# A down projection made of seven quarter products instead of eight, with VectorE summing the weights

## The chip, the cores and the metric

The kernel runs on one core of one Trainium2 chip. The metric is the device time of one execution in microseconds (us). Five engines work side by side, each through its own queue in order: TensorE (PE, matrix products), VectorE (DVE), ScalarE (ACT), GpSimd (POOL) and SyncE (SP), which here issues all the transfers.

## The reference, cut to what matters

One decoder layer on 512 tokens of 1024 channels: a combined projection, retention, dilated attention, a gated mix, an output projection, then the part that is changed:

```python
u = rmsnorm(x, g_mlp) @ w_up                  # w_up:   1024 x 4096
x = x + jnp.square(jax.nn.relu(u)) @ w_down   # w_down: 4096 x 1024
gate_p = jax.nn.sigmoid(rmsnorm(x, g_ple) @ w_ple_gate)
return x + gate_p * (p_i @ w_ple_proj)
```

All is float32.

## The kernel before

Every large product is made of three: each operand is split exactly into two parts of type float32r, `hi` and `lo`, and `mm3` issues hi·hi, hi·lo and lo·hi into one PSUM bank. One `mm3` is three matmuls of 128 x 128 stationary against 512 moving columns (fp32r), each with its own weight load (PEld in the profile).

**Weights.** `make_plan` lists 0.5 MB units of weights in the order of use. `fetch` takes a buffer of the pool `wraw` (three of them) and issues the transfer on SP. `split_unit` makes `whi` (ACT, a copy, L186) and `wlo` (DVE, raw minus whi, L187), both from the pool `wsp`, which has four buffers of each. `units(n)` hands out n units and has two more split ahead (`AHEAD`). So a unit's ACT copy waits until PE has left the unit four before it, and a transfer waits until an earlier unit's `wlo` has been made.

**The tail.** `tail` runs the output projection (w_o), then eight steps f of 512 hidden channels. Step f makes the up projection in two panels of 256 channels (`cols_gemm`: weights stationary, h2, the normed tokens, moving; 48 matmuls for two units), and then the down projection of step f-1 (`rows_gemm`, twice, for 512 output columns each: hidden values `uh`, `ul` stationary, weights moving; 48 matmuls for two units). So the values of a step are used one step after they are made. The function `act` turns a PSUM bank of 128 channels into hidden values: relu on ACT, times itself on DVE, `uh` on ACT, `ul` on DVE. A finished down bank is added to the tokens `x` by DVE (`add`, L835), one bank of 128 tokens x 512 columns at a time. In the last step the tokens go on into `norm_T` as they come: squares with row sums on ACT, a power on POOL, a scaling on DVE (`y`), four PE transposes each for two halves, and for each 128 channels a scaled copy on ACT (`h3h`) and a difference on DVE (`h3l`). The gate product (w_ple_gate) reads these.

**Order.** The code is recorded by a framework that schedules the instructions of each engine by their priority and by when buffers come free, so the size of a pool can move instructions anywhere in the program. Transposes of the norm are put into a list with a lag and are issued between steps of products (`later`, `tick`).

**Memory.** Large tiles come from `bigp`, 16 buffers of 128 x 2048 floats. PSUM has two pools of four banks, `psg` (`gbank`) and `psa` (`bank`).

Of the kernel before, what the change touches and what calls it, by code (L numbers as in the profile page):

```python
# [71 lines left out]
def R(ap):  # L72
    return ap.bitcast(F32R)


class Block:
    """One decoder layer on one core."""

    def __init__(self, ctx, tc, a):
        self.tc, self.nc, self.a = tc, tc.nc, a  # L80
        pool = lambda n, b, **k: ctx.enter_context(tc.tile_pool(name=n, bufs=b, **k))
        self.const = pool("const", 1)
        self.wraw = pool("wraw", 3)
# [17 lines left out]
    def later(self, lag, fn, key=None):  # L101
# [44 lines left out]

# [1 line left out]
    AHEAD = 2  # L148

    def plan_rows(self, w, c0, nk, r0=0):  # L150
        for u in range(nk // 2):
            self.plan.append((w[r0 + 256 * u : r0 + 256 * (u + 1), c0 : c0 + 512], 2 * u if w is self.w_in else None))

    def plan_cols(self, w, c0, nk):
# [3 lines left out]
    def fetch(self, n):  # L158
        while len(self.raws) < min(len(self.plan), n):
            src, g0 = self.plan[len(self.raws)]  # L160
            raw = self.wraw.tile([P, 1024], F32, tag="raw", name=self.nm("raw"))
            k = src.shape[0] // P
            raw = raw.rearrange("p (k n) -> p k n", k=k)
            self.nc.sync.dma_start(raw, src.rearrange("(k p) n -> p k n", p=P))
            self.raws.append((raw, g0))

    def ahead(self, n):
        while len(self.loaded) < min(len(self.plan), self.used + n):
            self.fetch(len(self.loaded) + 1)
            self.loaded.append(self.split_unit(*self.raws[len(self.loaded)]))  # L170

# [6 lines left out]
    def split_unit(self, raw, g0):  # L178
        """raw weights (times the gain of their input channel) as the exact sum of two float32r parts"""
        nc = self.nc  # L180
        k = raw.shape[1]
        hi = self.wsp.tile([P, 1024], F32, tag="whi", name=self.nm("whi")).rearrange("p (k n) -> p k n", k=k)
        lo = self.wsp.tile([P, 1024], F32, tag="wlo", name=self.nm("wlo")).rearrange("p (k n) -> p k n", k=k)
        if g0 is None:
            for i in range(k) if self.pinned else [slice(0, k)]:
                self.pin(nc.scalar.activation(R(hi[:, i]), raw[:, i], AF.Copy))  # L186
                nc.vector.tensor_tensor(R(lo[:, i]), raw[:, i], hi[:, i], op=ALU.subtract)  # L187
        else:
            for i in range(k):
                g = self.gcol[:, g0 + i : g0 + i + 1]  # L190
                self.pin(nc.scalar.activation(R(hi[:, i]), raw[:, i], AF.Copy, scale=g))  # L191
# [23 lines left out]

    def mm3(self, ps, sh, sl, mh, ml, first, last):
        t = self.nc.tensor
        t.matmul(ps, sh, mh, start=first, stop=False)  # L218
        t.matmul(ps, sh, ml, start=False, stop=False)  # L219
        t.matmul(ps, sl, mh, start=False, stop=last)  # L220
# [91 lines left out]

# [1 line left out]
    def rstd(self, ss, w, count):  # L314
# [47 lines left out]

# [1 line left out]
    def setup(self):  # L364
# [62 lines left out]

# [1 line left out]
    def embed(self, norm):  # L429
# [31 lines left out]

# [215 lines left out]

# [1 line left out]
    def ret_proj(self, extra=None):  # L679
# [97 lines left out]

# [1 line left out]
    def mix(self, A, O):  # L779
# [43 lines left out]

# [1 line left out]
    def tail(self, mx):  # L825
# [21 lines left out]
        h3 = None  # L847
        us = {}
        for f in range(NF + 1):
            if f < NF:  # L850
                u = self.new_act(1, "u")
                us[f] = u

                def act(n, ps):
                    r, q = self.tmp("ur"), self.tmp("uq")
                    nc.scalar.activation(r, ps, AF.Relu)
                    nc.vector.scalar_tensor_tensor(q, ps, 0.0, r, op0=ALU.max, op1=ALU.mult)
                    hi, lo = u[0][0][:, n], u[1][0][:, n]
                    nc.scalar.activation(R(hi), q, AF.Copy)
                    nc.vector.tensor_tensor(R(lo), q, hi, op=ALU.subtract)  # L860

                if f == 0:
                    self.cols_gemm_halves(h2, KD, act, lambda t: self.force(("h2", t, 1)))
                else:
                    for c in range(2):
                        self.cols_gemm(h2, KD, lambda n, ps: act(2 * c + n, ps))
            if f == 2:
# [4 lines left out]
            if f > 0:  # L872
                ub = us.pop(f - 1)
                for half in range(2):
                    cons = add(half)
                    if f == NF and half == 1:
                        h3 = self.new_act(2, "h3")

                        def cons(t, ps):
                            add(1)(t, ps)  # L880
                            self.norm_T(xs[t], t, 24, h3, "h3", 3)
                    self.rows_gemm(ub, 4, cons)

# [12 lines left out]
    def make_plan(self):  # L896
# [9 lines left out]
        for half in range(2):  # L906
            self.plan_rows(a["w_o"][0], 512 * half, KD)
        for f in range(NF + 1):
            if f < NF:
                for c in range(2):  # L910
                    self.plan_cols(a["w_up"][0], 512 * f + 256 * c, KD)
            if f > 0:
                for half in range(2):
                    self.plan_rows(a["w_down"][0], 512 * half, 4, 512 * (f - 1))
        for half in range(2):
# [37 lines left out]
```

## Time and profile before

| what | value |
| --- | --- |
| median of 3 runs | 1062.81 us (1061.33 to 1064.92) |
| profiled execution, first to last instruction (span) | 1058.8 us |
| PE busy in the span | 1033.6 us (98%) |
| DVE, ACT, POOL busy | 587.3, 425.5, 137.7 us |
| granted TensorE clock, mean | 0.998 |
| read from HBM, written | 98.61 MB, 4.21 MB |
| tail with the eight steps | from about 652 to 1008 us of the span |

The record gives the profiled execution by its span; its time as a run is not listed beside it. The median of the runs is 4.0 us above the span. A profile line names the line of the code, the engine, the operation, what is written and read (buffer numbers left out), the shape, and how many; then the busy time, the mean of one in ns, and the idle time of the engine just before, with what ended it. An x and a count after an engine's time is the number of instructions. A timeline line has the start and the duration in us.

### The profile page before, as it was taken

Reading aid. Unit: us, or ns where it says so; the run is one execution under the profiler, and the core shown is the slowest. Engines: PE = TensorE matmul, PEld = TensorE weight load, DVE = VectorE, ACT = ScalarE, POOL = GpSimd, SP = SyncE. Lnnn points to the kernel's source line nnn. Section 1 sums busy time; section 2 is a strip of 40 time slices with the busy share of each in tenths; the row PEclk is TensorE's granted clock in tenths of the full one; section 3 lists DMA queues with packets and bytes.
Section 4 is the critical chain, followed back from the end, with each engine's and each line's share of the span. In section 5 each row is a group of like instructions: output and inputs, shape, how many; then the busy total and the mean of one; then the engine's idle time right before and its main releaser. Section 6 shows DMA issues by size and latency. Waiting matters only on the chain.

```text
span 1058.8 us, 12846 instructions
## 1 busy us (share of the span) xinstructions
PE 1033.6 (98%) x4906; PEld 866.1 (82%) x4906; DVE 587.3 (55%) x929; ACT 425.5 (40%) x948; POOL 137.7 (13%) x126
## 2 busy tenths in 40 slices
PE   8898989999998999999999999999999999999998
PEld 6776879989986888888888888988888888888887
DVE  5588767677578635545443436554444545445573
ACT  6444545555533334435333325532232332332351
POOL 0254034033025301010100100000000000000000
PEclk9999999999999999999999999999999999999999
DMA  8432312223221322212234332225232332323221
GB/s 305 133 114 72 94 41 80 80 80 100 80 80 40 119 80 74 86 60 86 93 100 133 135 107 72 91 82 197 80 119 80 99 101 85 114 88 110 81 80 59
DMA packets 71708, 103.64 MB, mean 98 GB/s; under 512 B 5808, under 2 KB 38624, under 8 KB 71648
## 3 DMA queue, kind: packets, MB, share of 16 engines
q1 hardware_dynamic: 71648, 102.83, 30.8%
q8 instruction: 38, 0.62, 0.2%
q14 instruction: 22, 0.18, 0.1%
HBM read 98.61 MB, written 4.21 MB: 97 GB/s over the span
## 4 chain that ended last, share of the span: by engine, by line
PE 82%; DVE 6%; issue 2%; POOL 2%; ACT 1%; DMA 1%; DVEq 0%; ACTq 0%; POOLq 0%
PE pg L218 25%; PE pg L219 25%; PE pg L220 25%; DVE ro L472 2%; DVE wlo L192 1%; PE ph L484 1%; POOL r L317 1%; PE pt L327 1%; POOL mt L667 1%; PE po L600 1%; PE sc L577 1%; DVE ro L474 1%; PE ry L762 1%; DVE zn L520 1%; DMA raw<-in_w_up 1%
## 5 line engine op out<-in xcount | busy, mean ns | idle before, releaser
L218 PE MATMUL pg<-whi,hh 128*128 128x512 f32 x480 | 201.0, 419 | 3.2 <-ACT whi L191 2.2
L219 PE MATMUL pg<-wlo,hh 128*128 128x512 f32 x480 | 189.0, 394 | 1.7 <-DVE wlo L192 1.6
L220 PE MATMUL pg<-whi,hl 128*128 128x512 f32 x480 | 189.1, 394 | 0.0
L186 ACT ACTIVATE whi<-raw 128x1024 fp32r<-128x1024 f32 (+1 forms) x96 | 99.8, 1041 | 177.0 <-PE pg L220 117.0
L187 DVE TENSOR_TENSOR wlo<-raw,whi 128x1024 fp32r<-128x1024 f32 (+1 forms) x96 | 118.4, 1235 | 87.6 <-ACT whi L186 86.7
L192 DVE SCALAR_TENSOR_TENSOR wlo<-raw,gcol,whi 128x512 fp32r<-128x512 f32 (+1 forms) x184 | 122.2, 705 | 64.3 <-ACT whi L191 64.1
L191 ACT ACTIVATE whi<-raw,gcol 128x512 fp32r<-128x512 f32 (+1 forms) x184 | 107.6, 640 | 90.2 <-PE pg L220 51.4
L317 POOL TENSOR_TENSOR r<-v,mhalf 128x1 f32<-128x1 f32 (+1 forms) x52 | 40.4, 777 | 672.3 <-DVE v L316 672.3
L218 PEld LDWEIGHTS pg<-whi,hh 128*128 128x128 f32 x480 | 98.5, 205 | 17.9 <-ACT whi L191 2.8
L219 PEld LDWEIGHTS pg<-wlo,hh 128*128 128x128 f32 x480 | 99.0, 206 | 16.8 <-DVE wlo L192 3.3
L220 PEld LDWEIGHTS pg<-whi,hl 128*128 128x128 f32 x480 | 98.3, 205 | 17.4 <-DVE hl L341 0.4
L218 PE MATMUL pg<-h2h,whi 128*128 128x512 f32 (+1 forms) x288 | 105.7, 367 | 1.7 <-ACT h2h L335 1.7
L219 PE MATMUL pg<-h2l,whi 128*128 128x512 f32 (+1 forms) x288 | 105.3, 366 | 0.0
L220 PE MATMUL pg<-h2h,wlo 128*128 128x512 f32 (+1 forms) x288 | 105.2, 365 | 0.0
L218 PE MATMUL pg<-whi,uh 128*128 128x512 f32 x256 | 99.9, 390 | 0.0
L220 PE MATMUL pg<-whi,ul 128*128 128x512 f32 x256 | 99.6, 389 | 0.0
L219 PE MATMUL pg<-wlo,uh 128*128 128x512 f32 x256 | 99.6, 389 | 0.0
L835 DVE TENSOR_TENSOR x<-x,pg 128x512 f32<-128x512 f32 x72 | 49.4, 686 | 65.3 <-PE pg L220 65.1
L218 PEld LDWEIGHTS pg<-h2h,whi 128*128 128x128 f32 x288 | 54.3, 188 | 10.7 <-ACT h2h L335 1.9
L219 PEld LDWEIGHTS pg<-h2l,whi 128*128 128x128 f32 x288 | 54.3, 189 | 8.9 <-DVE h2l L336 0.2
L220 PEld LDWEIGHTS pg<-h2h,wlo 128*128 128x128 f32 x288 | 54.3, 188 | 8.7
L220 PEld LDWEIGHTS pg<-whi,ul 128*128 128x128 f32 x256 | 48.0, 188 | 10.0
(159 smaller groups left out, 1644.3 us busy)
## 6 DMA issues: line engine op xcount, KB each, us to landing
raw<-in_w_in SPq DMA_DIRECT2D x76, 512.0 KB, 3.7
raw<-in_w_up SPq DMA_DIRECT2D x32, 512.0 KB, 3.8
raw<-in_w_down SPq DMA_DIRECT2D x32, 512.0 KB, 3.5
raw<-in_w_ret_out SPq DMA_DIRECT2D x8, 512.0 KB, 3.5
raw<-in_w_o SPq DMA_DIRECT2D x8, 512.0 KB, 3.4
raw<-in_w_ple_gate SPq DMA_DIRECT2D x8, 512.0 KB, 3.5
x<-in_x SPq DMA_DIRECT2D x8, 256.0 KB, 6.5
pp_dram<-pp SPq DMA_DIRECT2D x8, 256.0 KB, 3.5
```

Source lines behind the costliest of these rows:

```text
L186: self.pin(nc.scalar.activation(R(hi[:, i]), raw[:, i], AF.Copy))
L187: nc.vector.tensor_tensor(R(lo[:, i]), raw[:, i], hi[:, i], op=ALU.subtract)
L191: self.pin(nc.scalar.activation(R(hi[:, i]), raw[:, i], AF.Copy, scale=g))
L192: nc.vector.scalar_tensor_tensor(R(lo[:, i]), raw[:, i], g, hi[:, i], op0=ALU.mult, op1=ALU.subtract)
L218: t.matmul(ps, sh, mh, start=first, stop=False)
L219: t.matmul(ps, sh, ml, start=False, stop=False)
L220: t.matmul(ps, sl, mh, start=False, stop=last)
L317: self.nc.gpsimd.tensor_tensor(r, v, self.mhalf[:, :w], op=ALU.pow)
L327: nc.tensor.transpose(ps[:, k * P : (k + 1) * P], part[:, k * P : (k + 1) * P], self.ident)
L472: nc.vector.tensor_tensor(v4(t2)[:, :, o0 : o0 + 64], v4(zn)[:, :, i0 : i0 + 64], bc(Sn[:, o0 : o0 + 64], 64), op=ALU.mult)
L474: nc.vector.tensor_tensor(o, t1, t2, op=ALU.add)
L835: nc.vector.tensor_tensor(v, v, ps, op=ALU.add)
```

## The change

The loop over eight steps becomes a loop over four of 1024 hidden channels. The up projection of a step is four panels of 256 channels as before, in another order. Its down projection is 512 tokens x 1024 channels times 1024 channels x 1024 columns; both operands are halved both ways, and the four quarters of the result are put together from seven quarter products (a scheme of the Strassen kind, in Winograd's form) in place of eight. Each quarter product is 256 tokens x 512 channels x 512 columns, 24 matmuls, for two units of weights.

The left sides are made by `seven_left` once for each 128 channels of half a step: with z the four squared quarters, four DVE differences (one of 512 elements, three of 256), one ACT copy and one DVE difference of 1792 elements for hi and lo. The right sides are weight units; products 4, 3, 7 and 6 need the sum of two quarters (two transfers and a DVE sum for each unit, L205), product 1 the difference of two units that are already loaded (L202), products 5 and 2 a plain unit. So a step's down projection loads 20 units of `w_down` where it loaded 8, makes 14 units where it had 8, and DVE makes 10 sums or differences of 128 x 1024. The order of the units is m4 m3 m5 m4 m3 m5, m2 m2, m1 m1, m7 m7, m6 m6, with two PE banks for each, and products 2, 7 and 6 are summed onto the banks of 4, 5 and 3. The banks go into `x` by 18 DVE additions of 128 x 512 per step; there were 16 for the same channels. The relu is squared by ACT (it was a DVE product). Down now follows up directly within a step. `wraw` has six buffers in place of three; the scratch for dynamic transfers is made smaller.

```diff
-        self.wraw = pool("wraw", 3)
+        self.wraw = pool("wraw", 6)
...
+    def seven_left(self, z, a21, U, j):
+        sub = lambda o, x, y: nc.vector.tensor_tensor(o, x, y, op=ALU.subtract)
+        sub(z[:, 2], z[:, 1], z[:, 0])
+        sub(z[:, 3:5], z[:, 0:2], z[:, 7:8].to_broadcast([P, 2, 256]))
+        sub(z[:, 5], a21, z[:, 7])
+        sub(z[:, 6], a21, z[:, 1])
...
+        nc.scalar.activation(R(hi), src, AF.Copy)
+        nc.vector.tensor_tensor(R(lo), src, hi, op=ALU.subtract)
...
     def ahead(self, n):
...
+            if isinstance(src, tuple) and src[0] is None:
+                self.nc.vector.tensor_tensor(raw, raw, self.raws[g0][0], op=ALU.subtract)
+                g0 = None
+            elif isinstance(src, tuple):
+                self.nc.vector.tensor_tensor(raw, raw, g0, op=ALU.add)
+                g0 = None
+            self.loaded.append(self.split_unit(raw, g0))
...
+    def seven_gemm(self, U, xs, ready):
...
+        for u in range(2):
+            for m in (4, 3, 5):
+                product(m, m, u, u == 0, u == 1)
+        m4 = []
+        for p in range(2):
+            t = self.tmp("m4")
+            nc.scalar.activation(t, banks[4, p], AF.Copy)
+            m4.append(t)
+            acc(X(0, 1, p), banks[3, p])
+            acc(X(0, 1, p), banks[5, p], ALU.subtract)
+        for u in range(2):
+            product(2, 4, u, False, u == 1)
+        for p in range(2):
+            acc(X(1, 0, p), banks[4, p])
+            acc(X(1, 1, p), banks[4, p], ALU.subtract)
+        for u in range(2):
+            product(1, 1, u, u == 0, u == 1)
+        for p in range(2):
+            acc(m4[p], banks[1, p])
+            acc(X(0, 0, p), m4[p])
+            acc(X(1, 1, p), m4[p])
+        for u in range(2):
+            product(7, 5, u, False, u == 1)
+        for p in range(2):
+            acc(X(0, 0, p), banks[5, p])
+            if ready is not None:
+                ready(p)
+        for u in range(2):
+            product(6, 3, u, False, u == 1)
+        for p in range(2):
+            acc(X(1, 1, p), banks[3, p])
+            if ready is not None:
+                ready(2 + p)
...
-        for f in range(NF + 1):
+        for f in range(NF // 2):
...
+            self.seven_gemm(U, xs, ready)
```

How it moves instructions, at three places. First VectorE's queue in a down projection, before, from the first addition of a down projection of 512 channels into its second half of columns:

```order
L835 TENSOR_TENSOR x_5176<-x_5176,pg_7448 128x512
L860 TENSOR_TENSOR ul_7287<-uq_7431,uh_7286 128x512
L835 TENSOR_TENSOR x_5176<-x_5176,pg_7462 128x512
L835 TENSOR_TENSOR x_5177<-x_5177,pg_7476 128x512
L187 TENSOR_TENSOR wlo_7507<-raw_7504,whi_7506 128x1024
L835 TENSOR_TENSOR x_5177<-x_5177,pg_7490 128x512
L187 TENSOR_TENSOR wlo_7513<-raw_7510,whi_7512 128x1024
L835 TENSOR_TENSOR x_5176<-x_5176,pg_7516 128x512
```

and in the changed kernel, at the end of a down projection, products 1, 7 and 6 (`m_` is the copy of product 4, `raw` a weight unit, `pb` and `pg` banks):

```order
L900 TENSOR_TENSOR x_5177<-x_5177,m_7388 128x512
L224 TENSOR_TENSOR wlo_7486<-raw_7480,whi_7485 128x1024
L205 TENSOR_TENSOR raw_7501<-raw_7501,raw_7503 128x1024
L900 TENSOR_TENSOR x_5176<-x_5176,pb_7316 128x512
L900 TENSOR_TENSOR x_5176<-x_5176,pb_7323 128x512
L224 TENSOR_TENSOR wlo_7507<-raw_7501,whi_7506 128x1024
L224 TENSOR_TENSOR wlo_7527<-raw_7524,whi_7526 128x1024
L224 TENSOR_TENSOR wlo_7545<-raw_7542,whi_7544 128x1024
```

Between two banks' additions now stand sums of weights and splits, and the split of product 6's second unit (`wlo_7507`) stands behind the additions of product 7's banks.

Second, PE's queue where the last down projection ends and the gate product begins, before (`uh` hidden values, `pt` transposes of `y`, `h3h` and `h3l` the gate's left side):

```order
L218 MATMUL pg_8068<-whi_7866,uh_7572 128x512
L219 MATMUL pg_8068<-wlo_7867,uh_7572 128x512
L220 MATMUL pg_8068<-whi_7866,ul_7573 128x512
L327 MATMUL pt_8110<-ident,y_8051 128x128 x4
L218 MATMUL pg_8135<-whi_7932,h3h_7926 128x512
L219 MATMUL pg_8135<-wlo_7933,h3h_7926 128x512
L220 MATMUL pg_8135<-whi_7932,h3l_7928 128x512
```

and now:

```order
L256 MATMUL pg_7928<-whi_8134,uh_7565 128x512
L257 MATMUL pg_7928<-wlo_8135,uh_7565 128x512
L258 MATMUL pg_7928<-whi_8134,ul_7569 128x512
L256 MATMUL pg_8301<-whi_8184,h3h_7888 128x512
L257 MATMUL pg_8301<-wlo_8185,h3h_7888 128x512
L258 MATMUL pg_8301<-whi_8184,h3l_7890 128x512
L256 MATMUL pg_8301<-whi_8184,h3h_7888 128x512
L257 MATMUL pg_8301<-wlo_8185,h3h_7888 128x512
L365 MATMUL pt_8244<-ident,y_8178 128x128 x4
```

Before, `pt_8110` is the third token tile's first half, and all transposes of the first two tiles stand ahead of it; now the gate's first matmul stands ahead of `pt_8244`, which is the first half of the second tile.

Third, the head of SP's queue, before:

```order
L384 DMA x_91<-in_x 128x512 x2
L164 DMA raw_98<-in_w_in 128x2x512
L384 DMA x_91<-in_x 128x512 x2
L164 DMA raw_102<-in_w_in 128x2x512
L372 DMA rows<-in_ret_gn 8x128
```

and now:

```order
L189 DMA raw_98<-in_w_in 128x2x512
L422 DMA x_91<-in_x 128x512 x2
L189 DMA raw_102<-in_w_in 128x2x512
L422 DMA x_91<-in_x 128x512 x2
L189 DMA raw_106<-in_w_in 128x2x512
```

With six buffers the weight transfers move ahead of the last token tiles and, further on, of other loads; between the head of the program and the tail PE's order stays the same.

More of the change, by code (lines that the diff above doesn't have):

```diff
@@ L160, in fetch @@
             src, g0 = self.plan[len(self.raws)]
+            add = None
+            if isinstance(src, tuple):
+                src, add = src[0], src[1:]
+            if src is None:
+                self.raws.append((self.raws[add[0]][0], add[1]))
+                continue
             raw = self.wraw.tile([P, 1024], F32, tag="raw", name=self.nm("raw"))
@@ L163, in fetch @@
             raw = raw.rearrange("p (k n) -> p k n", k=k)
-            self.nc.sync.dma_start(raw, src.rearrange("(k p) n -> p k n", p=P))
+            rows = lambda v: v.rearrange("(k p) n -> p k n", p=P)
+            self.nc.sync.dma_start(raw, rows(src))
+            if add is not None:
+                g0 = self.wraw.tile([P, 1024], F32, tag="raw", name=self.nm("raw2")).rearrange("p (k n) -> p k n", k=k)
+                self.nc.sync.dma_start(g0, rows(add[0]))
             self.raws.append((raw, g0))
@@ L168, in ahead @@
         while len(self.loaded) < min(len(self.plan), self.used + n):
-            self.fetch(len(self.loaded) + 1)
-            self.loaded.append(self.split_unit(*self.raws[len(self.loaded)]))
+            i = len(self.loaded)
+            self.fetch(i + 1)
+            raw, g0 = self.raws[i]
+            src = self.plan[i][0]
+            if isinstance(src, tuple) and src[0] is None:
[5 more added lines that the diff above has]
+            self.loaded.append(self.split_unit(raw, g0))
     def units(self, n):
@@ L214, in cols_gemm_halves, with mm3 @@
                     consume(n, banks[n])
-    def mm3(self, ps, sh, sl, mh, ml, first, last):
+    def mm3(self, ps, sh, sl, mh, ml, first, last, more=False):
         t = self.nc.tensor
-        t.matmul(ps, sh, mh, start=first, stop=False)
-        t.matmul(ps, sh, ml, start=False, stop=False)
-        t.matmul(ps, sl, mh, start=False, stop=last)
+        t.matmul(ps, sh, mh, start=first, stop=False, skip_group_check=more)
+        t.matmul(ps, sh, ml, start=False, stop=False, skip_group_check=more)
+        t.matmul(ps, sl, mh, start=False, stop=last, skip_group_check=more)
     def rows_gemm(self, act, nk, consume, perm=False, group=2, need=None, wave=None, halves=False):
@@ L822, in plan_mix @@
                     self.plan_cols(w, 256 * cc, nk)
+    def seven_left(self, z, a21, U, j):
+        nc = self.nc
+        sub = lambda o, x, y: nc.vector.tensor_tensor(o, x, y, op=ALU.subtract)
[3 more added lines that the diff above has]
+        sub(z[:, 6], a21, z[:, 1])
+        w = lambda t: t.rearrange("p a b -> p (a b)")[:, : 7 * 256]
+        hi, lo, src = w(U[0][j]), w(U[1][j]), z[:, 1:8].rearrange("p a b -> p (a b)")
+        nc.scalar.activation(R(hi), src, AF.Copy)
+        nc.vector.tensor_tensor(R(lo), src, hi, op=ALU.subtract)
@@ new lines, in seven_gemm, with product, acc @@
+    def seven_gemm(self, U, xs, ready):
+        nc = self.nc
+        LEFT = {1: 3, 2: 4, 3: 0, 4: 6, 5: 1, 6: 5, 7: 2}
+        banks = {}
+        def product(m, bank, u, first, last):
+            (wh, wl), = self.units(1)
+            for p in range(2):
+                if first:
+                    banks[bank, p] = self.gbank() if m in (3, 4) else self.bank("pb")
+                ps = banks[bank, p]
+                for k in range(2):
+                    kk = 2 * u + k
+                    c = slice(LEFT[m] * 256 + p * P, LEFT[m] * 256 + (p + 1) * P)
+                    sh, sl = (R(U[i][kk].rearrange("p a b -> p (a b)")[:, c]) for i in range(2))
+                    self.mm3(ps, sh, sl, wh[:, k], wl[:, k], first and k == 0, last and k == 1, m != bank)
+                self.tick()
+        X = lambda i, j, p: xs[2 * i + p][:, 512 * j : 512 * (j + 1)]
+        def acc(x, v, op=ALU.add):
+            nc.vector.tensor_tensor(x, x, v, op=op)
+        for u in range(2):
+            for m in (4, 3, 5):
[7 more added lines that the diff above has]
+            acc(X(0, 1, p), banks[5, p], ALU.subtract)
+        for u in range(2):
+            product(2, 4, u, False, u == 1)
+        for p in range(2):
+            acc(X(1, 0, p), banks[4, p])
+            acc(X(1, 1, p), banks[4, p], ALU.subtract)
+        for u in range(2):
+            product(1, 1, u, u == 0, u == 1)
[3 more added lines that the diff above has]
+            acc(X(1, 1, p), m4[p])
+        for u in range(2):
+            product(7, 5, u, False, u == 1)
[3 more added lines that the diff above has]
+                ready(p)
+        for u in range(2):
+            product(6, 3, u, False, u == 1)
+        for p in range(2):
+            acc(X(1, 1, p), banks[3, p])
+            if ready is not None:
+                ready(2 + p)
@@ L847, in tail, with act @@
         h3 = None
-        us = {}
-        for f in range(NF + 1):
[L850 to L863, printed above, removed]
-                else:
-                    for c in range(2):
-                        self.cols_gemm(h2, KD, lambda n, ps: act(2 * c + n, ps))
-            if f == 2:
+        for f in range(NF // 2):
+            U = [[self.big("uh") for _ in range(4)], [self.big("ul") for _ in range(4)]]
+            Z = {}
+            def act(b, j, ps):
+                r = self.tmp("ur")
+                nc.scalar.activation(r, ps, AF.Relu)
+                if b == 0:
+                    z = self.big("z").rearrange("p a (b t) -> p (a b) t", b=2)
+                    a21 = self.tmp("a21")[:, :256]
+                    Z[j] = z, a21
+                    nc.scalar.activation(z[:, 1], r[:, :256], AF.Square)
+                    nc.scalar.activation(a21, r[:, 256:], AF.Square)
+                else:
+                    z, a21 = Z[j]
+                    nc.scalar.activation(z[:, 0:8:7], r.rearrange("p (h t) -> p h t", h=2), AF.Square)
+                    self.seven_left(z, a21, U, j)
+            for jj in range(2):
+                if f == 0 and jj == 0:
+                    self.cols_gemm_halves(h2, KD, lambda n, ps: act(n // 2, n % 2, ps),
+                                          lambda t: self.force(("h2", t, 1)))
+                else:
+                    for b in range(2):
+                        self.cols_gemm(h2, KD, lambda n, ps: act(b, 2 * jj + n, ps))
+            if f == NF // 2 - 1:
                 pp = [self.big("pp") for _ in range(2)]
@@ L871, in tail @@
                         "(t p) n -> p t n", p=P))
[L872 to L882, printed above, removed]
+            ready = None
+            if f == NF // 2 - 1:
+                h3 = self.new_act(2, "h3")
+                ready = lambda t: self.norm_T(xs[t], t, 24, h3, "h3", 2 if t < 2 else 0)
+            self.seven_gemm(U, xs, ready)
         out = self.a["out"][0]
@@ L907, in make_plan @@
             self.plan_rows(a["w_o"][0], 512 * half, KD)
[L908 to L914, printed above, removed]
+        for f in range(NF // 2):
+            for jj in range(2):
+                for b in range(2):
+                    self.plan_cols(a["w_up"][0], 512 * (2 * f + b) + 256 * jj, KD)
+            self.plan_seven(a["w_down"][0], 1024 * f)
         for half in range(2):
```

12 lines of the change are left out of this document (11 added, 1 removed).

## The prediction

> **What bounds the kernel now.** I read the page's busy times first, then who waits for whom in the tail, then two stretches of the loop, then the spacing of the matmuls, and last the rows that price the new work.
>
> ```profile
> span 1058.8 us, 12846 instructions
> PE 1033.6 (98%) x4906; PEld 866.1 (82%) x4906; DVE 587.3 (55%) x929; ACT 425.5 (40%) x948; POOL 137.7 (13%) x126
> L218 PE MATMUL pg<-whi,uh 128*128 128x512 f32 x256 | 99.9, 390 | 0.0
> ```
>
> ```profile
> PE pg L218 <- ACT h2h L335: 1.7, 1, 1.7
> PE pt L327 <- DVE y L356: 0.8, 2, 0.5
> ```
>
> The second fence is all that PE waits for from 650 us to the end: 2.5 us. So the tail is PE's alone. The down projection has three groups like the third row above (L218, L219, L220): 768 matmuls.
>
> Two stretches of the loop show what the others do beside it (columns: window, its length, then PE, PEld, DVE, ACT, POOL busy with counts, granted clock, DMA share, GB/s):
>
> ```profile
> 820.00:864.00 44.00, 44.00 (x196) 36.44 (x195) 20.65 (x25) 13.19 (x16) 0.00 (x0) 1.00 0.32 96
> 864.00:907.00 43.00, 43.00 (x192) 35.59 (x191) 19.83 (x24) 13.19 (x16) 0.00 (x0) 1.00 0.32 98
> ```
>
> PE has no gap, the clock is full, DVE is under half busy. What a matmul is worth is not its duration but the distance to the next. The first and the last of the 196 matmuls that PE's timeline lists for this stretch:
>
> ```profile
> 863.61 0.39 PE L218 MATMUL pg<-h2h,whi 128*128 128x512 f32 x1
> ...
> 907.81 0.39 PE L218 MATMUL pg<-h2h,whi 128*128 128x512 f32 x1
> ```
>
> 44.20 us over 195 distances is 0.2267 us each, not 0.39: the durations overlap. [...] By durations the sum below would begin with 37.4 us, and the rows say that this is wrong.
>
> **The change part by part.**
>
> *Matmuls removed.* Each step of 1024 channels has 7 x 24 = 168 down matmuls for 8 x 24 = 192. Over four steps 96 go, on the path: 96 x 0.2267 = **21.8 us saved**. The up projections keep their count. [...] The row above has 0.2267 us in a stream without a gap, so I keep that.
>
> *Work added on DVE.* Prices, by form in the tail (count, busy, mean ns):
>
> ```profile
> L187 DVE TENSOR_TENSOR wlo<-raw,whi 128x1024 fp32r<-128x1024 f32 x55 | 67.3, 1224 | 57.7 <-ACT whi L186 57.7
> L186 ACT ACTIVATE whi<-raw 128x1024 fp32r<-128x1024 f32 x56 | 59.4, 1061 | 140.4 <-PE pg L220 106.8 <-PE pg L219 28.2 <-issue 5.4
> L835 DVE TENSOR_TENSOR x<-x,pg 128x512 f32<-128x512 f32 x63 | 43.2, 686 | 55.9 <-PE pg L220 55.9
> L891 DVE TENSOR_TENSOR fs<-fo,x 128x256 f32<-128x256 f32 x2 | 0.8, 425 | 0.1
> ```
>
> A sum of weights (f32 out) has no row. It reads and writes as much as a split, so I take the split's 1.22 us; a difference of 1792 elements follows from the slope between 512 and 1024 as 2.0 us. A step then costs DVE 32 x 1.22 (10 sums, 22 splits) + 22 x 0.69 (18 additions, 4 differences) + 12 x 0.43 + 4 x 2.0 = 67 us, for 360 x 0.2267 = 81.6 us of PE. Before, the two stretches above, together one such step, had 40.5 of 87. On average it is hidden. ACT gets 22 copies, 8 relus, squares and 4 wide copies: some 42 us, hidden too.
>
> But a step has two halves. The up half (43.5 us of PE) has room; the down half (38.1 us, 14 units of 12 x 0.2267 = 2.72 us) has nearly all sums and additions. There I lay DVE's queue end to end. Spacing of DVE instructions that have nothing to wait for:
>
> ```profile
> 842.51 1.23 DVE L187 TENSOR_TENSOR wlo<-raw,whi 128x1024 fp32r<-128x1024 f32 x1 [1.82 <-ACT whi L186]
> 843.66 0.68 DVE L835 TENSOR_TENSOR x<-x,pg 128x512 f32<-128x512 f32 x1
> 844.25 1.22 DVE L187 TENSOR_TENSOR wlo<-raw,whi 128x1024 fp32r<-128x1024 f32 x1
> 845.45 0.69 DVE L835 TENSOR_TENSOR x<-x,pg 128x512 f32<-128x512 f32 x1
> ```
>
> 1.15 to 1.20 us for 1024 elements, 0.59 us and up for 512: I take 1.17 and 0.63. How long a load takes to land (the tile's view, then the page):
>
> ```profile
> DMA to landing us min/median/max: 3.1/3.7/5.6
> GB/s 305 133 114 72 94 41 80 80 80 100 80 80 40 119 80 74 86 60 86 93 100 133 135 107 72 91 82 197 80 119 80 99 101 85 114 88 110 81 80 59
> ```
>
> Let the down half begin at 0. The first sum of product 7 needs two free buffers of six. The second comes free with the split of product 3's second unit, whose ACT copy waits until PE has left product 4's first unit: 2.72 + 0.16 (the tail of a 0.39 us matmul) + 1.06 + 1.15 = 5.1; landing 3.7 more: 8.8. From there to the split of product 6's second unit DVE has 14 instructions of 1024 (4 sums, 2 differences, 8 splits) and 16 additions: 14 x 1.17 + 16 x 0.63 = 26.5, done at 35.3. PE wants that split at 13 x 2.72 + 0.23 = 35.6. It is 0.3 us to spare, on a queue that also waits for banks on its way. Everything behind it on DVE (splits for the next up panel) and ACT (their copies) is late by as much, and PE waits for DVE. Upper end: instructions at full duration (14 x 1.22 + 16 x 0.69 = 28.1) and the slowest landing of 5.6: 38.8, or 3.2 us late. Lower end 0. I take **0.7 us a step, 2.8 us lost** (0 to 12.8), near the lower end, since the spacing is measured and the slowest landing is one load of many.
>
> The left sides: the last column's difference is made from banks that end at 0 and is wanted at 8.8 (product 4's second unit, its second 128 channels); relu, square, three differences, copy and difference are 0.6 + 0.6 + 1.5 + 1.7 + 2.0 and the queue ahead about 1.3, so 7.8. Hidden; a DVE delay of 1 us uncovers it.
>
> *Transfers.* 12 more loads a step on SP's queue, 25 MB in all. A step then moves 28 x 0.52 MB in 82 us, 180 GB/s, where the first slice of the page moved 305. SP issues each in 0.4 us and has nothing else there. Hidden, except through the buffers as above.
>
> *The way into the tail.* ACT's queue stands behind a late up load there, and with it h2:
>
> ```profile
> 656.20 1.06 ACT L186 ACTIVATE whi<-raw 128x1024 fp32r<-128x1024 f32 x1 [2.61 <-DMA raw<-in_w_up]
> 657.56 0.38 PE L218 MATMUL pg<-h2h,whi 128*128 128x256 f32 x1 [1.72 <-ACT h2h L335]
> ```
>
> With six buffers this load starts three loads earlier, so the wait goes: **1.7 us saved** (up to 2.6). Late next is the first sum of weights, which now stands in DVE's queue among h2's differences and waits for its own two loads: up to 2 us lost instead.
>
> *The way out.* The last step's tokens go through this chain (the chain that ended last):
>
> ```profile
> 997.79 0.68 DVE x L835
> 998.50 0.73 ACT j L350 x2
> ...
> 999.68 0.56 POOL r L317
> ...
> 1000.26 0.50 DVE y L356
> ...
> 1000.80 0.67 PE pt L327 x4
> ...
> 1001.49 0.37 ACT h3h L335
> ```
>
> From the addition to the first h3h end it is 4.1 us, then eight copies and differences of about 0.36 us a tile. Before, the first tiles were finished well ahead. Now tiles 0 and 1 get their last addition with product 7, one product (5.4 us) before the end, and h3h stands on ACT behind two gate copies (1.06 each) and the second tile's squares (0.63 each): the first comes about 1.4 us after PE is free, and the next ones arrive in another order than PE takes them. I take **3.5 us lost**; lower end 0.5 (as the wait above), upper end 6 (eight pairs of 0.36 + 0.35, each waited for).
>
> *The head of the program.* Loads are in another order there, and PE has a wait of its own:
>
> ```profile
> 40.48 0.50 PE L218 MATMUL pg<-whi,hh 128*128 128x512 f32 x1 [2.21 <-ACT whi L191]
> 42.00:46.00 4.00, 4.00 (x12) 3.13 (x12) 1.24 (x3) 2.53 (x12) 0.97 (x1) 0.57 0.42 133
> ```
>
> It waits for a weight load, and then runs 4 us at a clock of 0.57. If the wait goes, 2.2 + 4 x 0.43 = 3.9 us come back; if the load has to share with others, a landing of 3.7 is lost. Its place in SP's queue, behind the same small loads, is unchanged: 0, with both ends. [...]
>
> *Sum:* -21.8 - 1.7 + 2.8 + 3.5 + 0 = -17.2 us. On the span 1041.6; the runs' median lies 4.0 us above the span, and I carry that over: 1062.8 - 17.2 = **1045.6 us**.
>
> **The rivals.**
> - *DVE just too slow.* The upper end in every step, 12.8 us for 2.8: 1055.6. For it: 0.3 us to spare. Against it: the overlap is in the rows. 0.15.
> - *Slower: the sums wait for their buffers.* DVE works in order; where each sum of products 7 and 6 finds its second half still on the way, every split, addition and PE unit behind it waits. At 1.9 us (5.6 for 3.7) for four sums a step that is 7.6 us, 30 us in all: 1062.8 - 23.5 + 3.5 + 30 = 1073. It decides from 5 us a step on (20 / 4). For it: six buffers hold four operands for product 1. Against it: in my walk only the first sum waits. 0.11.
> - *No new waits.* 0 in the steps, 0.5 at the end, 2.6 at the way in, and the head's 3.9 come back: 1062.8 - 21.8 - 2.6 + 0.5 - 3.9 = 1035. 0.10.
> - *A matmul is worth less than its spacing.* If half of the 0.2267 us belonged to something that stays, which the profile doesn't show, 10.9 us go for 21.8: 1056.5. Against it: the stream has no gap, at full clock, and no other engine is near its limit in it. 0.02. [...]
>
> **How the numbers follow.** The forecast has 0.62 (1039 to 1052); the rivals as given. The range from 1036 to 1060 leaves out the slower rival and the outer part of the one without waits. Faster by over 0.3% (3.2 us, about what a measurement of this kernel can tell from no change): 0.62 + 0.10 + 0.02 and 0.09 of the 0.15, 0.83; within 0.3%: 0.06; slower 0.11.
>
> **What the profile would show.** Right: 672 down matmuls at 0.2267 us; DVE near 67 us in 82 of a step, and in a down half without idle time from its first sum on; PE's waits in a step only at product 6, on `wlo`, under 1 us; ACT's wait for an up load at the way in gone; 3 to 4 us of waits on h3h at the end. Wrong: PE waits of several us on `whi` or `wlo` with DVE waiting for loads; sums that take longer than a split; a lower clock after such waits; a head that moved by more than 1 us.

## The result, and the profile after

The changed kernel takes 1038.1 us (median of 4 runs, 1036.8 to 1038.7) where the kernel before takes 1062.3 us (1061.3 to 1064.9) beside it: a ratio of 0.9775, 95% interval 0.9756 to 0.9794, 24.2 us less. The forecast was 1045.6 us, 7.5 us more than measured; the time lies inside the range. A second set of runs gave 1036.7 against 1062.0 us, ratio 0.9763 (0.9741 to 0.9785).

The page's busy times, as they answer to those of before:

```profile
span 1036.7 us, 12913 instructions
PE 1014.2 (98%) x4810; PEld 848.4 (82%) x4810; DVE 676.6 (65%) x1017; ACT 480.4 (46%) x1012; POOL 137.8 (13%) x126
```

PE has 96 instructions fewer and is busy 19.4 us less; DVE is busy 89 us more. All that PE waits for from 650 us to the end (columns: the sum, how often, the longest):

```profile
PE pt L365 <- DVE y L394: 0.3, 1, 0.3
```

Not one wait on a weight, a sum or an `h3h`. Next the second step by windows, with the columns of the prediction: its down half, the up half behind it, and the stretch from the first sum of product 7 on.

```profile
781.75:819.83 38.08, 38.08 (x169) 31.54 (x168) 37.26 (x41) 18.18 (x19) 0.00 (x0) 1.00 0.59 189
819.83:863.35 43.52, 43.52 (x193) 36.05 (x192) 25.81 (x31) 21.93 (x30) 0.00 (x0) 1.00 0.53 174
791.00:819.00 28.00, 28.00 (x125) 23.17 (x125) 27.88 (x33) 11.43 (x13) 0.00 (x0) 1.00 0.66 210
```

38.08 us is 168 x 0.2267 and 43.52 is 192 x 0.2267: PE loses nothing. DVE is busy 63.1 of 81.6 us in a step, but 27.9 of 28.0 from the first sum on. So the engine that makes the sums is full for three quarters of a down half and PE still never waits. How near to the edge that is, DVE's timeline shows at the first and at the last of the four sums of products 7 and 6, and then PE's rows for the unit that needs the last one:

```profile
791.04 1.22 DVE L205 TENSOR_TENSOR raw<-raw,raw 128x1024 f32<-128x1024 f32 x1
...
813.34 1.21 DVE L205 TENSOR_TENSOR raw<-raw,raw 128x1024 f32<-128x1024 f32 x1
814.48 1.27 DVE L900 TENSOR_TENSOR x<-x,pb 128x512 f32<-128x512 f32 x2
815.76 3.50 DVE L224 TENSOR_TENSOR wlo<-raw,whi 128x1024 fp32r<-128x1024 f32 x3
```

```profile
817.11 0.39 PE L256 MATMUL pg<-whi,uh 128*128 128x512 f32 x1
817.34 0.39 PE L257 MATMUL pg<-wlo,uh 128*128 128x512 f32 x1
```

The first of the three splits ends at about 815.76 + 1.2 = 816.96; PE wants it at 817.34. That is some 0.4 us early, 35.2 us into the half; the walk in the prediction had 35.3 done for 35.6 wanted. That the ends agree to 0.1 us is in part luck. The walk lets the first sum start when its second load lands, at 8.8 us. The load does land then (at 790.56), but the sum stands behind a split and starts at 791.04, 9.3 us into the half. The queue from there on, with just the 14 instructions and 16 additions of the walk, takes 25.9 us where the walk had 26.5. The two errors cancel.

The way into the tail, PE in the same window of before and of after:

```profile
650.00:660.00 10.00, 8.28 (x58) 7.40 (x58) 7.12 (x15) 5.88 (x15) 0.41 (x1) 1.00 0.54 160
```

```profile
650.00:660.00 10.00, 10.00 (x72) 9.30 (x72) 9.63 (x22) 7.43 (x19) 1.46 (x1) 1.00 0.58 171
```

The gap of 1.7 us is gone, and ACT has no wait for an up load there any more. The way out, PE and then ACT:

```profile
982.03 0.66 PE L365 MATMUL pt<-ident,y 128*128 128x128 f32 x4 [0.30 <-DVE y L394]
982.76 0.60 PE L365 MATMUL pt<-ident,y 128*128 128x128 f32 x4
984.59 0.39 PE L256 MATMUL pg<-whi,h3h 128*128 128x512 f32 x1
```

```profile
982.86 0.62 ACT L388 ACTIVATE j<-x 128x512 f32<-128x512 f32 x1
...
983.47 0.35 ACT L373 ACTIVATE h3h<-pt,gcol 128x128 fp32r<-128x128 f32 x1
```

The first `h3h` starts 1.1 us before the gate's first matmul wants it.

The head: the wait of 2.21 us is down to 0.59, and no half clock follows it. But this execution ran at half clock twice elsewhere, from 151.3 and from 342.5 us, for 3.4 us each by the trace's clock records (windows around the first, with PE, PEld, DVE, ACT, POOL, granted clock, DMA share, GB/s):

```profile
38.80 0.49 PE L256 MATMUL pg<-whi,hh 128*128 128x512 f32 x1 [0.59 <-ACT whi L228]
```

```profile
148.00:152.00 4.00, 1.93 (x14) 1.64 (x13) 2.29 (x3) 0.20 (x1) 2.91 (x2) 0.91 0.00 0
152.00:156.00 4.00, 4.00 (x13) 3.19 (x12) 0.00 (x0) 0.40 (x1) 0.00 (x0) 0.66 0.00 0
```

Starts of the same PE instructions in the two traces, set beside each other, give the account of the 22.1 us of span: the changed kernel is 2.9 us ahead at 50 us, 1.8 us ahead from 75 to 145 us, 1.2 us behind at 640 us (the two half-clock stretches cost 1.8 and 1.6 us), 1.1 us ahead at 658 us, and 22.2 us ahead at the last matmul.

### The profile page after: what moved, and what is told of

Read it like the earlier page. It is cut to its first block, busy times and chain, and to the rows that moved or that the text cites. A ratio compares the mean times of both kernels' runs of the same rounds, so it can differ in the third digit from the quotient of the medians.

```text
span 1036.7 us, 12913 instructions
## 1 busy us (share of the span) xinstructions
PE 1014.2 (98%) x4810; PEld 848.4 (82%) x4810; DVE 676.6 (65%) x1017; ACT 480.4 (46%) x1012; POOL 137.8 (13%) x126
## 4 chain that ended last, share of the span: by engine, by line
PE 81%; DVE 8%; issue 2%; POOL 2%; ACT 1%; DMA 0%; DVEq 0%; ACTq 0%; POOLq 0%
PE pg L256 23%; PE pg L258 23%; PE pg L257 23%; DVE ro L510 2%; PE pb L256 2%; PE pb L258 2%; PE pb L257 2%; DVE wlo L224 1%; PE ph L522 1%; DVE wlo L229 1%; PE pt L365 1%; POOL r L355 1%; PE po L638 1%; PE sc L615 1%; DVE ro L512 1%
## 5 line engine op out<-in xcount | busy, mean ns | idle before, releaser
L223 ACT ACTIVATE whi<-raw 128x1024 fp32r<-128x1024 f32 (+1 forms) x120 | 123.6, 1043 | 131.9 <-PE pg L257 39.0
L224 DVE TENSOR_TENSOR wlo<-raw,whi 128x1024 fp32r<-128x1024 f32 (+1 forms) x120 | 146.2, 1230 | 36.8 <-ACT whi L223 35.7
L256 PE MATMUL pg<-hh,whi 128*128 128x512 f32 x128 | 52.4, 410 | 0.0
L257 PE MATMUL pg<-wlo,uh 128*128 128x512 f32 x128 | 50.1, 391 | 0.0
L258 PE MATMUL pg<-hh,wlo 128*128 128x512 f32 x128 | 50.0, 391 | 0.0
L257 PE MATMUL pg<-hl,whi 128*128 128x512 f32 x128 | 49.9, 390 | 0.0
L258 PE MATMUL pg<-whi,ul 128*128 128x512 f32 x128 | 49.9, 390 | 0.0
```

Of the source, the lines that this page charges most:

```text
L256: t.matmul(ps, sh, mh, start=first, stop=False, skip_group_check=more)
L257: t.matmul(ps, sh, ml, start=False, stop=False, skip_group_check=more)
L258: t.matmul(ps, sl, mh, start=False, stop=last, skip_group_check=more)
```

## The experiments

The kernel before ran beside each set of four: medians 1061.9, 1062.0 and 1062.0 us, so times of different sets can stand in one table; the changed kernel's own medians, 1038.1 and 1036.7, differ by 1.4 us between sets, and smaller differences between sets tell nothing. All are medians; the step is the distance between the first down matmuls of two steps.

| kernel | us | ratio to before, 95% | one step, us |
| --- | --- | --- | --- |
| changed, second set | 1036.7 | 0.9741 to 0.9785 | 81.6 to 81.7 |
| before, six buffers and the smaller scratch | 1059.2 | 0.9960 to 0.9985 | |
| 24 matmuls a step more | 1058.0 | 0.9946 to 0.9979 | 87.04 |
| sums left out | 1035.9 | 0.9736 to 0.9783 | 81.60 |
| DVE + 1 a step | 1041.2 | 0.9790 to 0.9826 | 82.6 to 82.9 |
| DVE + 2 | 1046.2 | 0.9844 to 0.9881 | 83.8 to 84.1 |
| DVE + 3 | 1052.1 | 0.9897 to 0.9932 | 85.0 to 85.3 |
| DVE + 4 | 1066.6 | 1.0028 to 1.0060 | 88.9 to 90.2 |
| DVE + 4, 24 matmuls more | 1061.3 | 0.9980 to 1.0010 | 87.04 |
| all sums on GpSimd | 1045.6 | 0.9829 to 0.9871 | 82.4 to 85.0 |
| sums of 4 and 3 on GpSimd | 1036.7 | 0.9756 to 0.9798 | 81.6 to 82.5 |
| five buffers | 1038.2 | 0.9762 to 0.9807 | 81.8 to 82.4 |

**The changed kernel again.**

> The changed kernel unaltered, as the measure for the runs beside it: 1038.1 us, with the same 81.6 us a step. The stretches of half clock between 140 and 350 us may fall elsewhere (each some 1.6 us).

1036.7 us. Its half-clock stretches lay at 70 and 340 us.

**The buffers without the seven products**, in the kernel before:

```diff
-        self.wraw = pool("wraw", 3)
+        self.wraw = pool("wraw", 6)
...
-    nc = bacc.Bacc("TRN2", target_bir_lowering=False, num_devices=1)
+    nc = bacc.Bacc("TRN2", target_bir_lowering=False, num_devices=1, dynamic_dma_scratch_size=4096)
```

> The kernel before with six weight buffers in place of three and the smaller scratch; eight products stay. Theory A (a part of the gain comes from the buffers alone): the wait of 2.21 us at the head shrinks to about 0.6 and the ACT wait for an up load at the way into the tail goes (the PE wait of 1.72 us with it), so 1062.3 - 1.6 - 2.2 = about 1058.5 us, down to 1057 if the half-clock stretch behind the head's wait goes too. Theory B (all of the gain is the 96 matmuls; the buffers only keep the sums fed): 1062 +- 1 us.

1059.2 us: 2.7 us less than before (1061.9), with an interval clear of 1. Theory A holds: a ninth of the change's gain has nothing to do with seven products. From 640 us to the end, PE's only wait is the 0.8 us on `y` that the kernel before has too; the one on `h2h` is gone. The run has the smaller scratch too, so it does not show what each of the two does alone.

**As many matmuls as with eight products, nothing else** (a part of product 1 is multiplied three times; the second pair of lines only allows the framework a bank that is begun anew):

```diff
-                for k in range(2):
+                for k in (0, 1, 0, 1, 0, 1) if m == 1 and u == 0 else (0, 1):
...
-                    self.mm3(ps, sh, sl, wh[:, k], wl[:, k], first and k == 0, last and k == 1, m != bank)
+                    self.mm3(ps, sh, sl, wh[:, k], wl[:, k], first and k == 0, last and k == 1, m != bank or m == 1)
```

> The changed kernel with 24 more matmuls in each step: the first weight unit of product 1 is multiplied three times into its banks, each time begun anew, so that the result stays and PE has the 96 matmuls back. Nothing else is added. Theory A (a matmul is worth its spacing): 1038.1 + 96 x 0.2267 = 1059.9 us. Theory B (a part of each step is set by DVE or the loads, so that more PE work is partly hidden): 1045 to 1055 us. Half the spacing: 1049 us.

1058.0 us, 21.3 more than the changed kernel. The first down matmul of two steps, here and then in the changed kernel:

```profile
784.72 0.39 PE L256 MATMUL pg<-whi,uh 128*128 128x512 f32 x1
...
871.76 0.39 PE L256 MATMUL pg<-whi,uh 128*128 128x512 f32 x1
```

```profile
781.75 0.39 PE L256 MATMUL pg<-whi,uh 128*128 128x512 f32 x1
...
863.35 0.39 PE L256 MATMUL pg<-whi,uh 128*128 128x512 f32 x1
```

87.04 and 81.60 us: 5.44 a step is 24 x 0.2267 to the last digit. PE waits for nothing in the tail. Theory A.

**The sums left out** (loads kept):

```diff
-                self.nc.vector.tensor_tensor(raw, raw, self.raws[g0][0], op=ALU.subtract)
...
-                self.nc.vector.tensor_tensor(raw, raw, g0, op=ALU.add)
```

> The changed kernel with the ten sums and differences of weights a step left out (the loads stay; the products then multiply plain quarters, so the result is another). DVE has 11.7 us less to do in a step. Theory A (DVE just fits, and all it does is hidden): no change, 1038.1 +- 1 us, DVE about 48 us busy fewer, PE without waits in the steps. Theory B (the sums cost something that the waits of PE don't show): 1030 to 1036 us.

1035.9 us, 0.8 below the changed kernel, which is within the spread of the runs (1035.0 to 1038.6). DVE has 45 us less:

```profile
PE 1011.4 (98%) x4810; PEld 846.7 (82%) x4810; DVE 632.0 (61%) x977; ACT 482.2 (47%) x1012; POOL 138.9 (13%) x126
```

So the ten sums and differences a step are hidden whole.

**More work for DVE**, one, two, three and four instructions a step (here four; the others change the set of units):

```diff
+        self.late.update(range(n + 10, n + 14))
...
+                if i in self.late:
+                    self.nc.vector.tensor_tensor(g0, g0, g0, op=ALU.max)
                 self.nc.vector.tensor_tensor(raw, raw, g0, op=ALU.add)
```

> The same with one more DVE instruction a step, ahead of the last sum only (product 6's second unit). Theory A (0.4 us to spare): 1.14 - 0.4 = 0.75 us a step, 3.0 in all: 1041.1 us. Theory B (slack of more than 1.2 us): 1038.1 us, no PE wait. Theory C (lateness runs on): 1043 us and more.

> Two more DVE instructions of 128 x 1024 a step, ahead of the two sums of product 6. With one the steps took 1.0 to 1.3 us longer each. Theory A (each further one adds its 1.14 us to the wait, and waits of 1 to 2 us leave the clock alone): 2.2 us a step, 8.8 in all: about 1045.5 us. Theory B (such a wait also halves the clock for some 16 matmuls, 3 us each time): 1057 us.

> Three more a step, ahead of all sums of products 7 and 6 but the first. Theory A (no half clock behind waits of 2.5 to 3 us): 3.3 us a step, 1050 us. Theory B (half clock behind each, as with four, where a step lost 7.3 to 8.6 us for 4.5 of work): 3.3 + 3 us a step, 1062 us.

> The changed kernel with four more DVE instructions of 128 x 1024 in each step, one ahead of each sum of products 7 and 6 (the maximum of a loaded unit with itself, which leaves it as it is). Theory A (DVE's queue is full in a down half and the split of product 6's second unit comes only 0.4 us before PE wants it): each step loses 4 x 1.14 - 0.4 = 4.2 us, 16.6 in all: 1054.7 us, with PE waiting on wlo or whi at products 7 and 6. Theory B (the queue has slack, since DVE waits 11 us for loads in the tail and order can give way): under 4 us lost, 1038 to 1042 us. Theory C (lateness runs on through the buffers into the next step): more than 20 us lost, above 1058 us.

One instruction of 1.14 us lengthens a step by 1.0 to 1.2 us, where Theory A had 0.75. The 0.4 us of the step above was not there to use, since the order of the queue shifts: one of the additions of product 7's banks now stands ahead of the last sum, and PE waits mostly for the ACT copy (`whi`) of that sum. Theory A's 1041.1 us was met by luck: it adds 3.0 us to 1038.1, and the runs are 4.5 us above 1036.7. Two and three follow the line (2.2, 3.4 us a step), as Theory A of those runs has it. With four the step loses 7.3 to 8.6 us, far off the line, and Theory A's 1054.7 us is missed by 12. Theory C's time is right, but lateness does not run on, which was its reason: PE waits in each step at one place, product 6 (with four instructions at its first unit). PE there in the third step, and the windows behind it:

```profile
910.26 0.39 PE L261 MATMUL pb<-whi,ul 128*128 128x512 f32 x1
914.11 1.22 PE L259 MATMUL pg<-whi,uh 128*128 128x512 f32 x2 [3.46 <-ACT whi L226]
915.81 0.79 PE L260 MATMUL pg<-wlo,uh 128*128 128x512 f32 x1 [0.48 <-DVE wlo L227]
916.40 0.63 PE L261 MATMUL pg<-whi,ul 128*128 128x512 f32 x1
916.83 0.63 PE L259 MATMUL pg<-whi,uh 128*128 128x512 f32 x1
```

```profile
914.00:918.00 4.00, 3.41 (x7) 2.31 (x8) 4.00 (x6) 3.01 (x4) 0.00 (x0) 0.50 0.95 297
918.00:922.00 4.00, 4.00 (x13) 3.10 (x13) 2.19 (x3) 1.06 (x1) 0.00 (x0) 0.66 1.04 343
922.00:926.00 4.00, 4.00 (x20) 3.30 (x19) 3.31 (x4) 1.06 (x1) 0.00 (x0) 1.00 0.84 276
```

Waits of 3.46 + 0.48 us, and 8 us at a mean clock of 0.50 and 0.66, in which the distance from matmul to matmul is 0.43 us for 6.8 us (half clock from 913.89 to 920.72 by the trace's clock records): 4 x 0.50 + 4 x 0.34 = 3.4 us more. Together about 7.3, which is what this step lost (88.88 - 81.60); the second wait lies inside the stretch, so how the loss divides is good to a few tenths of a us only. All four steps show 6.8 us of half clock. With three instructions the waits of a step are 0.5 and 1.5 us, and one of four was followed by half clock, for 3.4 us; so their line is nearly straight.

**The same four with more PE work.**

> The four DVE instructions a step and the 24 repeated matmuls of product 1 together. The repeated matmuls give DVE 5.44 us more time ahead of products 7 and 6, which is more than the 4.5 us by which it was late. Theory A (the 28 us of the four instructions are PE's waits and the half clock behind them): both go, and the time is that of the repeated matmuls alone, 1058 us, 8 us less than with fewer matmuls. Theory B (the four instructions cost by themselves, whatever PE does): 1066.6 + 20 = 1087 us.

1061.3 us: with 96 matmuls more the kernel is 5.3 us faster than with the four instructions alone. PE has no wait in the steps, and each takes 87.04 us, as without the four. Theory A's mechanism holds; its 1058 was missed by 3.3 us, of which the trace places 2.4 at the way out, where PE waits on `y` (0.9), on `h3h` (0.7) and behind `v` (0.5). `y` and `v` stand in the fuller queue of DVE; `h3h` stands on ACT behind the squares of the second tile.

**The sums on GpSimd**, all ten (shown), and then only the four of products 4 and 3:

```diff
-                self.nc.vector.tensor_tensor(raw, raw, self.raws[g0][0], op=ALU.subtract)
+                self.nc.gpsimd.tensor_tensor(raw, raw, self.raws[g0][0], op=ALU.subtract)
...
-                self.nc.vector.tensor_tensor(raw, raw, g0, op=ALU.add)
+                self.nc.gpsimd.tensor_tensor(raw, raw, g0, op=ALU.add)
```

> The changed kernel with the ten sums and differences a step on GpSimd in place of VectorE. POOL's rows of 128 x 512 are 1.04 to 1.50 us, so a sum is some 2.1 to 3.0 us, 21 to 30 us a step on an engine that stands idle in the steps. Theory A (hidden, as the sum no longer stands behind DVE's queue): 1038.1 +- 1 us, and DVE's queue gets room. Theory B (the sum is so much longer, or slows DVE so much, that products 7 and 6 wait): 1 to 5 us a step lost, 1042 to 1058 us, with more by half clock where a wait is above 2 us.

> The four sums of products 4 and 3 on GpSimd, which are made while the up projection runs; the other four sums and the two differences stay on VectorE. With all ten on GpSimd a split took 1.57 us in the mean for 1.22 and 8.9 us were lost. Theory A (GpSimd slows VectorE, but this costs only where VectorE's queue is full, in the down half): 1037 +- 1.5 us, with longer splits in the up half. Theory B (the loss goes with the number of sums on GpSimd): 4/10 of 8.9, 1040 us and more.

All ten: 1045.6 us, 8.9 lost, although DVE was relieved of 49 us of sums: Theory B. PE waits 4.3 us for `wlo` in the steps and 3.1 us for `y` at the way out. The 2 us from which that theory has half clock behind a wait was the author's estimate: behind the 3.09 us for `y` the granted clock was 1.00 from 988 to 992 us. The splits grew, in the tail of the changed kernel and of this one:

```profile
L224 DVE TENSOR_TENSOR wlo<-raw,whi 128x1024 fp32r<-128x1024 f32 x96 | 115.8, 1220 | 14.1 <-ACT whi L223 13.8
```

```profile
L224 DVE TENSOR_TENSOR wlo<-raw,whi 128x1024 fp32r<-128x1024 f32 x96 | 149.7, 1574 | 19.5 <-ACT whi L223 19.1
L205 POOL TENSOR_TENSOR raw<-raw,raw 128x1024 f32<-128x1024 f32 x32 | 84.8, 2650 | 211.9 <-DMA raw<-in_w_down 170.9 <-DVE wlo L224 23.1 <-ACT z L975 12.2
L202 POOL TENSOR_TENSOR raw<-raw,raw 128x1024 f32<-128x1024 f32 x8 | 22.7, 2858 | 4.7 <-DVE wlo L224 4.7
```

How a single one grows, POOL's row and then DVE's:

```profile
799.56 2.40 POOL L202 TENSOR_TENSOR raw<-raw,raw 128x1024 f32<-128x1024 f32 x1
```

```profile
797.27 1.27 DVE L900 TENSOR_TENSOR x<-x,pg 128x512 f32<-128x512 f32 x2
800.73 2.31 DVE L224 TENSOR_TENSOR wlo<-raw,whi 128x1024 fp32r<-128x1024 f32 x1 [2.19 <-ACT whi L223]
```

GpSimd's difference ends at 801.96; the split that began at 800.73 ends at 803.04, 1.08 us later, about its own length in the changed kernel (1.22). By these ends it did not run slowly but stood still until GpSimd's instruction was over. So it is with all 21 splits of the tail that began while GpSimd was at work: each ends 1.08 or 1.09 us after GpSimd's instruction, the longest takes 3.43 us. The 13 splits that began first took 1.21 to 1.23 us, and GpSimd's instruction ended 2.2 to 2.3 us behind them. DVE's differences of `z` grow too: those of 256 elements take 0.76 and 1.05 us in the mean where they took 0.42. The two additions at 797.27, whose second operand is a PSUM bank, took 1.27 us together, as in the changed kernel, while GpSimd was busy from 796.29 to 801.96. Why the splits stand still and these additions do not, the rows do not show.

Only the four early sums: 1036.7 us, no loss. The mean split of the tail takes 1.28 us for 1.22; four splits stood still, all in up halves, where DVE has room (busy 25.8 of 43.5 us in the changed kernel). Theory A of that run.

**Five buffers.**

```diff
-        self.wraw = pool("wraw", 6)
+        self.wraw = pool("wraw", 5)
```

> The changed kernel with five weight buffers in place of six. Theory A (the first sum of product 7 waits for its second free buffer, which comes one unit of 2.72 us later, and only 0.4 us is to spare): some 2.3 us a step lost, 1047 us. Theory B (a buffer is free in time, or the order gives way): 1038.1 +- 1 us. Theory C (loads run one unit late all through the step and PE waits several times a step): above 1055 us.

1038.2 us, 1.5 above the changed kernel in the same set, with overlapping runs (1036.9 to 1041.7 for 1035.5 to 1037.7). Theory A fell. The scheduler moved matmuls of the next up panel in between product 6's, which leaves the last split more time; the steps are 0.2 to 0.8 us longer and PE's waits in the tail add up to 0.9 us. The count of buffers decides less than the walk in the prediction had it.

None of the runs beats the changed kernel beyond its spread: in the tail PE has nothing left to wait for.

## Why the prediction was right, and where its terms were off

The direction, the main mechanism (removed matmuls are worth their spacing, and the work put on DVE is hidden) and the range of 1036 to 1060 us held. The new waits that the sum charged did not come, so the time lies just below the 1039 to 1052 us that the prediction thought likeliest. Term by term:

| term of the sum | forecast | measured | from |
| --- | --- | --- | --- |
| 96 matmuls | -21.8 | -21.8 | 4 x (87.04 - 81.60) in the run with 24 matmuls a step more |
| way into the tail | -1.7 | -2.25 | same PE instructions, from +1.18 at 640 us to -1.07 at 658 us |
| DVE late at product 6 | +2.8 | +0.1 | step lengths of 81.73, 81.60, 81.60 |
| way out | +3.5 | +0.5 | from the first matmul of the last down projection to the last matmul, without the down matmuls: 48.7 before, 49.2 after |
| head | 0 | about -0.5 | the rest: 2.7 us in the run with six buffers, less the 2.25 |

These add up to -24.0; the medians of the runs give -24.2. The two losses of the forecast, at product 6 and at the way out, were put 2.7 and 3.0 us too high; that makes 5.7 of the 7.5 us by which it was too long.

- *Matmuls.* Right: 0.2267 us each in this float32r stream, by the experiment (5.44 us for 24) as well as by the rows.
- *DVE at product 6: the step that failed is the charge, not the walk.* The walk gave 0.3 us to spare; the trace has 0.4 (with two errors of 0.5 us in the walk that cancel). Then 0.7 us a step was charged "near the lower end" for what the walk did not contain. No run of the changed kernel shows a wait there. The claim that PE would wait at product 6, on `wlo`, under 1 us, is wrong in the changed kernel; the kernel with one instruction more does wait there, but mostly on `whi`. DVE is busy 63 us in a step for the 67 of the prediction, which added up durations where the distances are shorter.
- *Way out: a mis-sized term, at its lower end.* The prediction had product 7's additions 5.4 us before the end of product 6. Between them PE now also makes the eight transposes of the first tile: product 6 lasts from 977.59 to 984.59, 7.0 us, and the chain from the addition at 977.96 to the end of `h3h` at 983.82 fits inside it. PE takes the gate's parts with transposes in between, and only fractions of a us are lost. The 3 to 4 us of waits on `h3h` that the prediction named as a sign of being right are not there.
- *Head.* Taken as 0 with both ends; the runs say a small gain. The prediction read a place in SP's queue and did not see that with three more buffers the queue gets there sooner: the load is issued at 26.7 us where it was 29.3, and its ACT copy starts at 38.0 where it was 39.7. The prediction named a head that moves by more than 1 us as a sign of being wrong, and at 50 us it has moved by 2.9. About 1.7 us of that is the half-clock stretch behind the head's wait, which the profile of before has and that of after has not; the changed kernel's stretches elsewhere take it back. What the smaller scratch alone is worth no run shows: the 2.7 us of the run with six buffers are of both.
- *The runs' time.* The 4.0 us between the span of before and the median of its runs was carried over. It stands on both sides of the forecast, so it does no harm there, but it is not one thing. For the changed kernel, the profiled execution took 1038.7 us for a span of 1036.7: 2.0 us. The record has span and granted clock of 43 more runs of before: their time is 1.7 to 1.9 us above their span, and the span goes with the clock (mean span 1058.1 us for the eight runs at 0.999 or 1.000, 1060.2 for 18 at 0.997, 1063.1 for seven at 0.995). So 1.8 of the 4.0 us belong to every run, and the other 2.2 go with more half clock in the median run than in the profiled one, which has one stretch. Profiles of one kernel show the stretches at different places (152 and 342 us, then 70 and 340).
- *No new waits.* This rival, with a chance of 0.10, was the nearest: 1035 us. Three of its four terms hold (nothing in the steps, 0.5 us at the way out, 2.6 at the way in for 2.25 measured); the 3.9 us of the head did not come back.
- *Slower rival.* Sums do wait for their loads (all of DVE's waits of that kind in the tail: sum, how often, the longest):

```profile
DVE raw L205 <- DMA raw<-in_w_down: 11.2, 12, 2.1
```

  But 11.0 of the 11.2 us are at the sums of products 4 and 3, which are made beside the up projection. Those of products 7 and 6, which the rival speaks of, wait once, for 0.2 us. That six buffers are too few is not borne out either: five do nearly as well.
- *DVE just too slow.* The rival was right about the edge: 0.4 us from it. With one more instruction of 1.14 us a step PE waits at product 6, as the rival said; its price of 3.2 us a step needs three.

## What to carry to other kernels

PE was all but without a gap here (2.5 us of waits from 650 us on), so the 96 matmuls removed were worth their spacing times their count (0.2267 us each, 21.8 us), and of the 89 us that the change put on DVE the steps showed 0.1. That held up to an edge, 0.4 us away by the trace: an end-to-end walk of DVE's queue, half by half, found the edge to a tenth of a us, with errors of 0.5 us that cancelled, and a charge for what the walk did not contain was wrong. Past the edge, each instruction cost about its full spacing of 1.14 us here (steps of 1.0 to 1.2, 2.2 and 3.4 us more with one to three), and with waits of PE of some 3.5 us 1.6 to 1.9 times that (7.3 to 8.6 us for 4.6), with half clock behind them. Ahead of such a change, try its side effects alone: here more buffers (and the smaller scratch) in the old kernel gave 2.7 us.

## What the hardware showed that was not expected

- *Some waits cost more than their length.* After each of four waits of 3.5 to 4.2 us the matmuls ran at 0.43 us apart for 6.8 us; in the step shown that was some 3.4 us on top of 3.9 of waiting. The stretches whose two ends the clock records of the kernel before (one) and of the changed kernel (two) show last 3.413 us each, and the changes of the clock lie whole multiples of that apart: 9, 1 and 297 before, 41, 1, 55 and 1 after. After the four waits of 1.5 us with three instructions more it happened once; the head of the kernel before has it behind 2.2 us. Two waits that the changes do not touch show how uncertain it is: the one of 2.0 us near 340 us was followed by half clock in 11 of the 14 profiles, the one of 1.9 to 2.1 us near 150 us in 4 of 14. And a wait of 3.1 us at the way out of the kernel with all sums on GpSimd was followed by a clock of 1.00 (PE's row, then the window behind it):

```profile
987.83 0.66 PE L365 MATMUL pt<-ident,y 128*128 128x128 f32 x4 [3.09 <-DVE y L394]
```

```profile
988.00:992.00 4.00, 4.00 (x25) 3.39 (x25) 3.33 (x9) 2.98 (x9) 0.55 (x1) 1.00 0.67 224
```

  So in these traces the length of a wait alone does not decide it: half clock stood behind one of 1.5 us and not behind one of 3.1. What does decide it they do not show.
- *More work, less time.* 96 matmuls added to the kernel with four DVE instructions a step took it from 1066.6 to 1061.3 us.
- *GpSimd as helper.* An idle engine made 40 sums in 107 us of its own time and cost 8.9 us; the 1.22 us splits of another engine stood still beside it and took up to 3.43.
